# Routing products in groups of eight tokens, all their 0/1 matrices made on VectorE

## The chip, the core and the metric

The kernel runs on one core of one Trainium2 chip. The metric is the device time of one execution in microseconds (us), taken as the median of several runs. Beside it stands one profiled execution, in which the start and the duration of every instruction were recorded; all rows below come from that one.

## The reference

The program computes two transformer blocks on 256 tokens of width 1024. Only the last part of the second block matters here, a mixture of 16384 small experts. For every token and each of 8 heads, two top-16 searches over 128 keys give candidate pairs, the best 16 pairs name experts by a first index `e // 128` and a second index `e % 128`, and a softmax gives each its weight g.

```python
def peer(xn, w_query, sub_keys, expert_u, expert_v):
    ...
        s1, i1 = lax.top_k(s[:, :, 0], PEER_TOPK)
        s2, i2 = lax.top_k(s[:, :, 1], PEER_TOPK)
        ...
        sc, ci = lax.top_k(cand, PEER_TOPK)
        e = (jnp.take_along_axis(i1, ci // PEER_TOPK, axis=-1) * N_KEYS
             + jnp.take_along_axis(i2, ci % PEER_TOPK, axis=-1))
        g = jax.nn.softmax(sc, axis=-1)
        u = expert_u[e]
        act = jax.nn.gelu(jnp.einsum('td,thkd->thk', xb, u).astype(jnp.float32))
        return jnp.einsum('thk,thkd->td', (g * act).astype(xb.dtype), expert_v[e])
```

## The kernel before

The kernel gathers no experts. It computes `gelu(x . u)` for all 16384 experts and all 256 tokens, multiplies by a weight that is zero for experts not chosen, and multiplies the result with all rows of `expert_v`. An f32 product is made of three TensorE passes over numbers split in two parts, a rounded part (`hh`, `wh`) and its remainder (`hl`, `wl`); that is `mm3`.

The work around the change, in order of time:

- **The expert_u units.** `expert_u` comes in 64 units of 256 experts, `u_unit(u)`. A unit has two halves; each half needs one raw 128x1024 tile from a DMA on SyncE's queue, a rounded copy `wh` by ScalarE (line 124) and a remainder `wl` by VectorE (line 130). Then TensorE runs 24 matmuls of 256 columns for each half into the PSUM tile `mid`, 48 a unit. `raw`, `wh` and `wl` have four buffers each, `mid` has two. After a unit, `u_done` applies gelu on ScalarE (line 1010) and stores to `acts0` (units 0 to 31) or `acts1` (units 32 to 63).
- **Routing.** During units 0 to 31 VectorE also ranks the keys. `select_(tb)` ends, for each 128 tokens, with the first index `f1` and the second index `f2` of each chosen expert (lines 938 to 941) and the weight `gw`; TensorE transposes the three (line 945), and ScalarE stores them as `key1`, `key2` and `gwt`, one column a token. `gwt` holds the weight as a sum of three bf16 parts.
- **The table.** `weighted()` is a generator that runs inside units 32 to 63: after every 12 matmuls the unit yields, and each time `next(table)` goes one step on, with one step more after every 12. For a token it makes two bf16 matrices over its 128 chosen pairs: `m2`, 1 where the second index equals the column, and `m1`, the weight where the first index equals the column (`eq`, the 0/1 matrix of line 1071, times `gwt`, line 1073). Three bf16 matmuls of 128 columns (one for each part of the weight), the products, give the token's 128x128 table of weights in a PSUM bank `acc` of four tokens. Of four bank-sized PSUM buffers `acc` in rotation each is emptied by VectorE, which multiplies it into `acts0` (line 1055) and into the units of `acts1` that are done (line 1058), and by ScalarE, which copies it to the units that are still to come (line 1060). Those are multiplied when the unit is done (lines 1012 and 1013).
- **Sizes before.** `eq` and `m1` are made for four tokens an operation. `m2` is made for one token an operation, for three tokens in four by GpSimd (line 1080, the compare in f32) and for the fourth by VectorE (line 1078). A step of the table issues the products of two tokens.
- **The expert_v units.** `v_units` multiplies the 64 units of `acts` with `expert_v`, into the four `acc` buffers.

TensorE's order is the order of the code: `in_line` chains all matmuls. On the other engines a scheduler sets the order from the program's dependences. `m1` and `m2` of a token are made ahead: 12 tokens of `m1` and 8 tokens of `m2` fit in their buffers.

Of the kernel before, what the change touches and what calls it, by code (L numbers as in the profile page):

```python
# [9 lines left out]
F32 = mybir.dt.float32  # L10
F32R = mybir.dt.float32r
BF16 = mybir.dt.bfloat16
I32 = mybir.dt.int32
U32 = mybir.dt.uint32
AF = mybir.ActivationFunctionType
OP = mybir.AluOpType
# [4 lines left out]
P = 128  # L21
S = 256
# [9 lines left out]
HALF = 32  # L32
WBUFS = 4
RBUFS = 4
GAP = 120

SCRATCH = 8192


C_CAUS = 0  # L40
# [39 lines left out]
def block_kernel(ctx: ExitStack, tc: tile.TileContext, a, out, dbg=None):  # L80
    nc = tc.nc
    vec, act, pe, pool = nc.vector, nc.scalar, nc.tensor, nc.gpsimd
# [60 lines left out]
    def matmul(p, x, y, start, stop):  # L143
        in_line(pe.matmul(p, x, y, start=start, stop=stop))  # L144
# [40 lines left out]
    def acc(shape):  # L185
        return ps.tile(shape, F32, name="acc", bufs=4)
# [4 lines left out]
    def tps(shape):  # L191
        return ps.tile(shape, F32, name="tps", bufs=2)
# [330 lines left out]
    i50, i128 = tok[:, :NCAND], tok[:, NCAND:]  # L523
# [18 lines left out]
    for bits in (8, 9, 9, 24):  # L542
        e = 2.0 ** (np.floor(np.log2(abs(rest))) - bits + 1)
        c = float(np.float32(np.round(rest / e) * e))
# [241 lines left out]
    for g0 in (0, 4):  # L786
        p = acc([P, 4, TB, 64])
        for gi in range(4):
            g = g0 + gi
# [3 lines left out]
    p = tps([P, TB, 2])  # L793
# [56 lines left out]
    ranked, done, keys = {}, set(), []  # L850
# [41 lines left out]
    def select_(tb):  # L892

        hv, hi = best[tb]
        hf = pq.tile([P, 8, 2, 16], F32, name="hf")
        turn_of(vec.tensor_scalar(hf[:, :, 0, :], hi[:, :, 0, :], 128.0, None, op0=OP.mult))
        vec.tensor_copy(hf[:, :, 1, :], hi[:, :, 1, :])
        cand = pq.tile([P, 8, NCAND], F32, name="cand")
        ecand = pq.tile([P, 8, NCAND], F32, name="ecand")
        for dst, src in ((cand, hv), (ecand, hf)):  # L900
            for o, i0, r, c in STAIR:
                i = vec.tensor_tensor(dst[:, :, o:o + r * c].rearrange("p h (r c) -> p h r c", c=c),
                                      src[:, :, 0, i0:i0 + r].unsqueeze(3).to_broadcast([P, 8, r, c]),
                                      src[:, :, 1, 0:c].unsqueeze(2).to_broadcast([P, 8, r, c]), op=OP.add)
            yield 2.0
        turns[0] = i
        sc = pq.tile([P, 8, 16], F32, name="sc16")
        pos = pq.tile([P, 8, 16], U32, name="pos")
        posf = pq.tile([P, 8, 16], F32, name="posf")
        ef = pq.tile([P, 8, 16], F32, name="ef")  # L910
        gw = pq.tile([P, 8, 16], F32, name="gw")
        gs = pq.tile([P, 8], F32, name="gs")
        for h in range(8):
            i = best16(sc[:, h, :], pos[:, h, :], cand[:, h, :], NCAND, True)
            if h % 2:
                turns[0] = i
                yield 1.8
        vec.tensor_tensor(gw, sc, sc[:, :, 0:1].to_broadcast([P, 8, 16]), op=OP.subtract)
        act.activation(gw, gw, AF.Exp)
        vec.tensor_copy(posf, pos)  # L920
        for h in range(0, 8, 2):
            eq = pq.tile([P, 2, 16, NCAND], F32, name="eq", bufs=1)
            shape = [P, 2, 16, NCAND]
            turn_of(vec.tensor_tensor(eq, i50.unsqueeze(1).unsqueeze(1).to_broadcast(shape),
                                      posf[:, h:h + 2, :].unsqueeze(3).to_broadcast(shape), op=OP.is_equal))
            yield 1.8
            vec.tensor_tensor(eq, eq, ecand[:, h:h + 2, :].unsqueeze(2).to_broadcast(shape), op=OP.mult)
            yield 1.8
            turns[0] = vec.tensor_reduce(ef[:, h:h + 2, :], eq, axis=AX.X, op=OP.add)
            yield 1.8  # L930
        vec.tensor_reduce(gs, gw, axis=AX.X, op=OP.add)
        vec.reciprocal(gs, gs)
        vec.tensor_tensor(gw, gw, gs.unsqueeze(2).to_broadcast([P, 8, 16]), op=OP.mult)
        ei = pq.tile([P, 8, 16], I32, name="ei")
        e1 = pq.tile([P, 8, 16], I32, name="e1")
        f1 = pq.tile([P, 8, 16], F32, name="f1")
        f2 = pq.tile([P, 8, 16], F32, name="f2")
        vec.tensor_copy(ei, ef)
        vec.tensor_scalar(e1, ei, 7, None, op0=OP.logical_shift_right)
        vec.tensor_copy(f1, e1)  # L940
        turns[0] = vec.scalar_tensor_tensor(f2, f1, -128.0, ef, op0=OP.mult, op1=OP.add)
        yield 2.0
        p = tps([P, 4, P])
        for n, src in enumerate((f1, f2, gw)):
            turn(p[:, n, :], src.rearrange("p h k -> p (h k)"))
        t = slice(tb * P, (tb + 1) * P)
        key1, key2, gwt = keys

        def twice(v):
            return v.unsqueeze(2).to_broadcast([P, P, 2])  # L950

        act.activation(key1[:, t, :], twice(p[:, 0, :]), AF.Copy)
        act.activation(key2[:, t], p[:, 1, :], AF.Copy)  # L953

        rest = pq.tile([P, 8, 16], F32, name="f1").rearrange("p h k -> p (h k)")
        act.activation(gwt[:, t, 0, :], twice(p[:, 2, :]), AF.Copy)
        vec.tensor_tensor(rest, p[:, 2, :], gwt[:, t, 0, 0], op=OP.subtract)
        act.activation(gwt[:, t, 1, :], twice(rest), AF.Copy)
        turns[0] = vec.tensor_tensor(rest, rest, gwt[:, t, 1, 0], op=OP.subtract)
        act.activation(gwt[:, t, 2, :], twice(rest), AF.Copy)  # L960
        yield 0.0
# [39 lines left out]
    acts = [pk.tile([P, 2 * HALF, S], F32, name="acts0")]  # L1001
    NU = NCHUNK // 2
    mixed_in = [0]
    gelus = [0]
# [11 lines left out]
    def u_unit(u):  # L1016
# [2 lines left out]

    abs_ = ExitStack()  # L1020
    ab = abs_.enter_context(tc.tile_pool(name="ab", bufs=1, reuse_waits="tile"))
    keys += [ab.tile([P, S, 2], BF16, name="key1"), ab.tile([P, S], F32, name="key2"),
             ab.tile([P, S, 3, 2], BF16, name="gwt")]
    key1, key2, gwt = keys
    i128b = ab.tile([P, P], BF16, name="i128b")
# [10 lines left out]
    acts.append(pk2.tile([P, 2 * HALF, S], F32, name="acts1"))  # L1036

    def weighted():
        ready = []
        banks = {}  # L1040

        def products(t, m1, m2):
            j = t // 4
            if t % 4 == 0:
                banks[j] = acc([P, 4, P])
            p = banks[j]
            for n in range(3):
                matmul(p[:, t % 4, :], m2, m1[:, n, :], n == 0, n == 2)
            if t % 4 < 3:
                return  # L1050
            ts = slice(4 * j, 4 * j + 4)
            k = 2 * (gelus[0] - HALF)
            pv = p.rearrange("p t c -> p c t")
            g = acts[0][:, :, ts]
            vec.tensor_tensor(g, g, pv[:, :P // 2, :], op=OP.mult)
            if k:
                g = acts[1][:, :k, ts]
                vec.tensor_tensor(g, g, pv[:, P // 2:P // 2 + k, :], op=OP.mult)
            if k < P // 2:
                act.activation(acts[1][:, k:, ts], pv[:, P // 2 + k:, :], AF.Copy)  # L1060
            mixed_in[0] = j + 1

        def by_twos(v):
            return v.rearrange("p t (k i) -> p t k i", i=2)

        for t in range(S):
            if t % 4 == 0:
                eq = ab.tile([P, 4, P], BF16, name="eq", bufs=1)
                m1 = ab.tile([P, 4, 3, P], BF16, name="m1", bufs=3)
                ts = slice(t, t + 4)  # L1070
                vec.tensor_tensor(by_twos(eq), by_twos(i128b.unsqueeze(1).to_broadcast([P, 4, P])),
                                  key1[:, ts, :].unsqueeze(2).to_broadcast([P, 4, P // 2, 2]), op=OP.is_equal)
                vec.tensor_tensor(m1.rearrange("p t n (k i) -> p t n k i", i=2),
                                  eq.rearrange("p t (k i) -> p t k i", i=2).unsqueeze(2).to_broadcast([P, 4, 3, P // 2, 2]),
                                  gwt[:, ts, :, :].unsqueeze(3).to_broadcast([P, 4, 3, P // 2, 2]), op=OP.mult)
            m2 = ab.tile([P, P], BF16, name="m2", bufs=8)
            if t % 4 == 3:
                vec.tensor_scalar(m2, i128b, key2[:, t:t + 1], None, op0=OP.is_equal)
            else:
                pool.tensor_scalar(m2, i128, key2[:, t:t + 1], None, op0=OP.is_equal)  # L1080
            ready.append((t, m1[:, t % 4], m2))
            if len(ready) > 4:
                products(*ready.pop(0))
            if t % 2:
                yield
        while ready:
            products(*ready.pop(0))
            if len(ready) % 2 == 0:
                yield

    table = weighted()
    steps = 0
# [10 lines left out]
    pv = late_pools.enter_context(tc.tile_pool(name="pv", bufs=1, reuse_waits="tile"))  # L1103
# [126 lines left out]
```

## Time and profile before

| | |
|---|---|
| runs, us | 1322.88, 1324.47, 1325.99 |
| median, us | 1324.47 |
| profiled execution, us | 1322.9, its span 1321.1 |
| TensorE clock granted, mean | 0.996 |
| busy: TensorE, VectorE, ScalarE, GpSimd | 97%, 71%, 52%, 31% |
| stage with products | 740 to 953 us of the span |

The span is the time from the first to the last instruction of the profiled execution; its own time is 1.8 us longer. A matmul's duration in the trace overlaps with its neighbours', so the pace of TensorE is read from the distance of two starts, not from durations. The same holds, to a lesser degree, for VectorE.

### The profile page before, as it was taken

What the parts mean: (1) busy time and instruction counts of PE and PEld (TensorE: products, weight loads), DVE (VectorE), ACT (ScalarE), POOL (GpSimd) and SP (SyncE); (2) the same over time, 40 slices, a digit from 0 to 9 for tenths busy, and PEclk for the clock granted to TensorE, in tenths of its full rate; (3) what the DMA queues carried; (4) which work ended last, traced back from release to release, by engine and by line L of the source; (5) the groups of instructions that cost most, each with busy time, mean ns of one, the idle gap of its engine ahead of it and who ended that gap; (6) DMA issues with size and microseconds to landing.
All of it is one profiled execution on the core that took longest, in us unless ns stands there. A gap on an engine that the chain in (4) does not pass through costs nothing.

```text
span 1321.1 us, 22724 instructions
## 1 busy us (share of the span) xinstructions
PE 1287.6 (97%) x8580; PEld 1144.6 (87%) x8580; DVE 932.0 (71%) x1924; ACT 682.7 (52%) x1046; POOL 405.4 (31%) x295
## 2 busy tenths in 40 slices
PE   6999999999998999999999999999999999999997
PEld 5788987899976777999999999999988888888885
DVE  6666777333357795799799699999955555555555
ACT  5576647455544655455564444444444444444443
POOL 3321335222244335300010499999700000000001
PEclk9999999999999999999999999999999999999999
DMA  8554565666645325456766544444476666666662
GB/s 287 169 174 129 183 201 168 215 192 191 191 139 188 113 80 178 126 155 181 226 188 197 172 145 146 147 142 149 154 231 195 194 192 193 194 195 195 194 192 81
DMA packets 64191, 230.65 MB, mean 175 GB/s; under 512 B 7280, under 2 KB 7696, under 8 KB 63952
## 3 DMA queue, kind: packets, MB, share of 16 engines
q1 hardware_dynamic: 61632, 221.03, 54.2%
q0 software_dynamic: 1728, 6.07, 1.3%
q10 hardware_dynamic: 720, 2.10, 0.4%
q8 instruction: 67, 1.10, 0.3%
q14 instruction: 44, 0.36, 0.1%
HBM read 227.07 MB, written 2.10 MB: 173 GB/s over the span
## 4 chain that ended last, share of the span: by engine, by line
PE 89%; DVE 5%; issue 3%; ACT 1%; DMA 1%; POOL 1%; SPq 0%; POOLq 0%; ACTq 0%; DVEq 0%
PE acc L144 52%; PE mid L144 35%; PE tps L154 2%; DVE wl L130 1%; DMA x<-in_x_dram 1%; POOL wl L130 1%; PE tps L144 1%; DVE cnat L339 0%; DVE rope_t L337 0%; DVE at_s L366 0%; ACT wh L124 0%; DVE ny L243 0%; DVE hl L183 0%; DVE rope_t L338 0%; DVE at_s L358 0%
## 5 line engine op out<-in xcount | busy, mean ns | idle before, releaser
L124 ACT ACTIVATE wh<-raw 128x1024 fp32r<-128x1024 f32 (+2 forms) x422 | 440.0, 1049 | 363.1 <-PE mid L144 161.8
L130 DVE TENSOR_TENSOR wl<-raw,wh 128x1024 fp32r<-128x1024 f32 (+1 forms) x350 | 443.7, 1269 | 216.4 <-ACT wh L124 214.0
L144 PE MATMUL mid<-hh,wh 128*128 128x256 f32 x1280 | 365.7, 286 | 0.0
L144 PE MATMUL mid<-hh,wl 128*128 128x256 f32 x1280 | 355.7, 278 | 0.0
L144 PE MATMUL mid<-hl,wh 128*128 128x256 f32 x1280 | 354.3, 277 | 0.0
L130 POOL TENSOR_TENSOR wl<-raw,wh 128x1024 fp32r<-128x1024 f32 (+3 forms) x72 | 177.5, 2475 | 323.9 <-ACT wh L124 273.0
L1080 POOL TENSOR_SCALAR m<-tok,key 128x128 bf16<-128x128 f32 x192 | 206.2, 1092 | 201.7 <-ACT key L953 120.4
L144 PEld LDWEIGHTS mid<-hl,wh 128*128 128x128 f32 x1280 | 241.2, 188 | 0.4
L144 PEld LDWEIGHTS mid<-hh,wh 128*128 128x128 f32 x1280 | 240.9, 188 | 0.4
L144 PEld LDWEIGHTS mid<-hh,wl 128*128 128x128 f32 x1280 | 240.4, 188 | 0.2
L144 PE MATMUL acc<-wl,ah 128*128 128x512 f32 x512 | 199.2, 389 | 0.0
L144 PE MATMUL acc<-wh,ah 128*128 128x512 f32 x512 | 199.2, 389 | 0.0
L144 PE MATMUL acc<-wh,al 128*128 128x512 f32 x512 | 199.2, 389 | 0.0
L144 PE MATMUL acc<-wh,hh 128*128 128x512 f32 (+2 forms) x288 | 115.8, 402 | 2.9 <-ACT hh L182 2.6
L144 PEld LDWEIGHTS acc<-wh,ah 128*128 128x128 f32 x512 | 96.1, 188 | 20.0
L144 PE MATMUL acc<-wl,hh 128*128 128x512 f32 (+2 forms) x288 | 112.2, 390 | 1.3 <-DVE wl L130 0.7
L144 PEld LDWEIGHTS acc<-wh,al 128*128 128x128 f32 x512 | 96.1, 188 | 20.0
L144 PEld LDWEIGHTS acc<-wl,ah 128*128 128x128 f32 x512 | 96.1, 188 | 19.8
L144 PE MATMUL acc<-wh,hl 128*128 128x512 f32 (+2 forms) x288 | 112.4, 390 | 0.8 <-DVE hl L183 0.6
L1138 POOL TENSOR_TENSOR hh<-hh,hl 128x512 f32<-128x512 f32 x4 | 5.1, 1284 | 344.9 <-ACT hl L1137 344.9
L182 ACT ACTIVATE ah<-acts 128x512 fp32r<-128x512 f32 x64 | 40.3, 632 | 88.8 <-PE acc L144 88.8
L183 DVE TENSOR_TENSOR al<-acts,ah 128x512 fp32r<-128x512 f32 x64 | 44.3, 693 | 52.0 <-ACT ah L182 52.0
(267 smaller groups left out, 1750.9 us busy)
## 6 DMA issues: line engine op xcount, KB each, us to landing
raw<-in_expert_u_dram SPq DMA_DIRECT2D x128, 512.0 KB, 3.8
raw<-in_expert_v_dram SPq DMA_DIRECT2D x128, 512.0 KB, 4.4
raw<-in_w_down_dram SPq DMA_DIRECT2D x32, 512.0 KB, 4.4
raw<-in_w_up_dram SPq DMA_DIRECT2D x24, 512.0 KB, 4.7
raw<-in_w_in_dram SPq DMA_DIRECT2D x20, 512.0 KB, 4.5
raw<-in_w_gate_dram SPq DMA_DIRECT2D x16, 512.0 KB, 4.6
raw<-in_w_out_dram SPq DMA_DIRECT2D x16, 512.0 KB, 4.4
raw<-in_w_in_n_dram SPq DMA_DIRECT2D x12, 512.0 KB, 4.5
```

The lines of the kernel that those rows point to most:

```text
L124: i = act.activation(h[:, :n], raw[:, :n], AF.Copy)
L130: last_split[0] = eng.tensor_tensor(l[:, :n], raw[:, :n], h[:, :n].bitcast(F32), op=OP.subtract)
L144: in_line(pe.matmul(p, x, y, start=start, stop=stop))
L154: in_line(pe.transpose(out, src, ident))
L182: turned_[0] = act.activation(h, p, AF.Copy)
L183: vec.tensor_tensor(l, p, h.bitcast(F32), op=OP.subtract)
L1080: pool.tensor_scalar(m2, i128, key2[:, t:t + 1], None, op0=OP.is_equal)
L1138: pool.tensor_tensor(y[:, tb, c], y[:, tb, c], gfin[:, c], op=OP.mult)
```

## The change

The table works in groups of eight tokens. VectorE makes the 0/1 matrices of all tokens, `eq` from `key1` and `m2` from `key2`, each in one operation of 8x128 columns for eight tokens, and `m1` in one operation of 8x384 columns; GpSimd has no part in it. `key2` is stored like `key1`, as bf16 with each value twice. A group's three operations stand in three steps of the table, a fourth step is empty, and the next group's first step issues the 24 products of the group before, back to back. `m1` and `m2` have two buffers of eight tokens, `eq` has one. The room for it comes from two sizes: `GAP`, a filler tile, and `SCRATCH`, the scratch space of the transfers that GpSimd issues.

```diff
-GAP = 120
-
-SCRATCH = 8192
+GAP = 8
+
+SCRATCH = 4096
...
-        act.activation(key2[:, t], p[:, 1, :], AF.Copy)
+        act.activation(key2[:, t, :], twice(p[:, 1, :]), AF.Copy)
...
-            for n in range(3):
-                matmul(p[:, t % 4, :], m2, m1[:, n, :], n == 0, n == 2)
-            if t % 4 < 3:
-                return
...
+        def products(t0, m1, m2):
+            for j in range(t0 // 4, (t0 + T) // 4):
+                p = acc([P, 4, P])
+                for t in range(4 * j, 4 * j + 4):
+                    for n in range(3):
+                        matmul(p[:, t % 4, :], m2[:, t - t0, :], m1[:, t - t0, n, :], n == 0, n == 2)
...
-            m2 = ab.tile([P, P], BF16, name="m2", bufs=8)
-            if t % 4 == 3:
-                vec.tensor_scalar(m2, i128b, key2[:, t:t + 1], None, op0=OP.is_equal)
-            else:
-                pool.tensor_scalar(m2, i128, key2[:, t:t + 1], None, op0=OP.is_equal)
-            ready.append((t, m1[:, t % 4], m2))
-            if len(ready) > 4:
-                products(*ready.pop(0))
-            if t % 2:
-                yield
...
+        def equal(dst, key, ts):
+            vec.tensor_tensor(by_twos(dst), by_twos(i128b.unsqueeze(1).to_broadcast([P, T, P])),
+                              key[:, ts, :].unsqueeze(2).to_broadcast([P, T, P // 2, 2]), op=OP.is_equal)
+
+        made = None
+        for t0 in range(0, S, T):
+            ts = slice(t0, t0 + T)
+            if made:
+                products(*made)
+            eq = ab.tile([P, T, P], BF16, name="eq", bufs=1)
+            equal(eq, key1, ts)
+            yield
+            m2 = ab.tile([P, T, P], BF16, name="m2", bufs=2)
+            equal(m2, key2, ts)
+            yield
+            m1 = ab.tile([P, T, 3, P], BF16, name="m1", bufs=2)
+            vec.tensor_tensor(m1.rearrange("p t n (k i) -> p t n k i", i=2),
+                              by_twos(eq).unsqueeze(2).to_broadcast([P, T, 3, P // 2, 2]),
+                              gwt[:, ts, :, :].unsqueeze(3).to_broadcast([P, T, 3, P // 2, 2]), op=OP.mult)
+            made = (t0, m1, m2)
+            yield
+            yield
+        products(*made)
+        yield
```

In the changed kernel the lines after the diff's first part are numbered differently: 1063 is `equal` (`eq` and `m2`), 1078 is `m1`, 1051, 1054 and 1056 are the three that were 1055, 1058 and 1060.

Over the whole program, TensorE's order before has 118 unbroken runs of products, 108 of six and 10 of twelve; afterwards it has 32 runs of 24. All other matmuls stand in the same order. On TensorE, in unit 33, the end of the first run of products before (`acc`, from `m1` and `m2`) and what follows it:

```order
L144 MATMUL acc_8256<-m1_8215,m2_8218 128x128
L144 LDWEIGHTS m2_8220
L144 MATMUL acc_8256<-m1_8215,m2_8220 128x128
L144 LDWEIGHTS m2_8220
L144 MATMUL acc_8256<-m1_8215,m2_8220 128x128
L144 LDWEIGHTS m2_8220
L144 MATMUL acc_8256<-m1_8215,m2_8220 128x128
L144 MATMUL mid_8201<-hh_4200,wh_8197 128x256
```

and, in the first run of the changed kernel, the place where the fourth token ends and the fifth begins:

```order
L144 MATMUL acc_8282<-m1_8242,m2_8228 128x128
L144 LDWEIGHTS m2_8228
L144 MATMUL acc_8282<-m1_8242,m2_8228 128x128
L144 LDWEIGHTS m2_8228
L144 MATMUL acc_8298<-m1_8242,m2_8228 128x128
L144 LDWEIGHTS m2_8228
```

Where the unit's matmuls (`mid`) came back after two tokens, the next bank's products now follow without a break.

On VectorE, in the middle of the stage with products, two rounds of the table before (1055 and 1058 empty a bank, 1078 is the fourth token's `m2`, 1073 is `m1`, 1071 is `eq`, 1013 is a unit's product, 130 is `wl`):

```order
L1055 TENSOR_TENSOR acts_5882<-acts_5882,acc 128x64x4
L1058 TENSOR_TENSOR acts_8188<-acts_8188,acc 128x18x4
L1078 TENSOR_SCALAR m_9444<-i128b,key_5887 128x128
L1073 TENSOR_TENSOR m_9465<-eq,gwt 128x1536
L130 TENSOR_TENSOR wl<-raw,wh 128x1024
L1071 TENSOR_TENSOR eq<-i128b,key_5886 128x512
L1013 TENSOR_TENSOR acts_8188<-mid,acts_8188 128x2x80
L1055 TENSOR_TENSOR acts_5882<-acts_5882,acc 128x64x4
L1058 TENSOR_TENSOR acts_8188<-acts_8188,acc 128x20x4
L1078 TENSOR_SCALAR m_9496<-i128b,key_5887 128x128
L1073 TENSOR_TENSOR m_9520<-eq,gwt 128x1536
L1071 TENSOR_TENSOR eq<-i128b,key_5886 128x512
```

and the same stretch now:

```order
L1051 TENSOR_TENSOR acts_5882<-acts_5882,acc 128x64x4
L1054 TENSOR_TENSOR acts_8188<-acts_8188,acc 128x18x4
L1063 TENSOR_TENSOR m_9296<-i128b,key_5887 128x1024
L1078 TENSOR_TENSOR m_9313<-eq,gwt 128x3072
L130 TENSOR_TENSOR wl<-raw,wh 128x1024
L1063 TENSOR_TENSOR eq<-i128b,key_5886 128x1024
L1013 TENSOR_TENSOR acts_8188<-mid,acts_8188 128x2x80
L1051 TENSOR_TENSOR acts_5882<-acts_5882,acc 128x64x4
L1054 TENSOR_TENSOR acts_8188<-acts_8188,acc 128x20x4
L130 TENSOR_TENSOR wl<-raw,wh 128x1024
L1051 TENSOR_TENSOR acts_5882<-acts_5882,acc 128x64x4
L1054 TENSOR_TENSOR acts_8188<-acts_8188,acc 128x20x4
```

The three table operations of eight tokens stand once for two bank emptyings, the two long ones together between two `wl`.

On VectorE too, but earlier, at the end of routing for the second 128 tokens, before (938 to 941 make the indices that TensorE transposes next):

```order
L929 TENSOR_REDUCE ef_7347<-eq_7909 128x32
L130 TENSOR_TENSOR wl_8063<-raw_8060,wh_8062 128x1024
L938 CAST ei_7978<-ef_7347 128x128
L130 TENSOR_TENSOR wl_8069<-raw_8066,wh_8068 128x1024
L939 TENSOR_SCALAR e1_7979<-ei_7978 128x128
L940 CAST f1_7980<-e1_7979 128x128
L941 SCALAR_TENSOR_TENSOR f2_7981<-f1_7980,ef_7347 128x128
L130 TENSOR_TENSOR wl_8125<-raw_8122,wh_8124 128x1024
L130 TENSOR_TENSOR wl_8131<-raw_8128,wh_8130 128x1024
```

and now:

```order
L929 TENSOR_REDUCE ef_7347<-eq_7909 128x32
L130 TENSOR_TENSOR wl_8069<-raw_8066,wh_8068 128x1024
L938 CAST ei_7978<-ef_7347 128x128
L130 TENSOR_TENSOR wl_8125<-raw_8122,wh_8124 128x1024
L939 TENSOR_SCALAR e1_7979<-ei_7978 128x128
L940 CAST f1_7980<-e1_7979 128x128
L941 SCALAR_TENSOR_TENSOR f2_7981<-f1_7980,ef_7347 128x128
L130 TENSOR_TENSOR wl_8131<-raw_8128,wh_8130 128x1024
```

The split `wl_8125` stood behind 941 and now stands ahead of 939. Between the indices of the first and of the second 128 tokens VectorE has 4 `eq` (four tokens each), 2 `m2` (one token each) and 3 `m1` (four tokens each) before, and 3 `eq`, 2 `m2` and 2 `m1`, all of eight tokens, now.

## Rows read from the trace of the kernel before

**Rows 1.** The page, part 1: busy us, share of the span, instructions.

```profile
PE 1287.6 (97%) x8580; PEld 1144.6 (87%) x8580; DVE 932.0 (71%) x1924; ACT 682.7 (52%) x1046; POOL 405.4 (31%) x295
```

**Rows 2.** Window with products: length, busy PE, PEld, DVE, ACT, POOL, clock, DMA, GB/s.

```profile
740.00:953.00 213.00, 213.00 (x2176) 208.79 (x2175) 202.50 (x396) 94.48 (x178) 200.93 (x186) 1.00 0.49 147
```

**Rows 3.** Waits between 740 and 953 us: total, times, longest.

```profile
ACT wh L124 <- PE mid L144: 73.8, 47, 2.4
ACT acts L1060 <- DVE acts L1058: 40.4, 28, 2.1
DVE acts L1055 <- PE acc L144: 7.7, 19, 1.3
```

**Rows 4.** Timeline of PE: start, duration; unit matmuls without and with products.

```profile
722.41 0.28 PE L144 MATMUL mid<-hh,wh 128*128 128x256 f32 x1
...
723.77 0.28 PE L144 MATMUL mid<-hh,wh 128*128 128x256 f32 x1
...
756.08 0.28 PE L144 MATMUL mid<-hh,wl 128*128 128x256 f32 x1
756.20 0.84 PE L144 MATMUL acc<-m,m 128*128 128x128 bf16 x12
756.85 0.36 PE L144 MATMUL mid<-hh,wh 128*128 128x256 f32 x1
...
758.20 0.28 PE L144 MATMUL mid<-hh,wl 128*128 128x256 f32 x1
...
758.64 0.36 PE L144 MATMUL mid<-hh,wh 128*128 128x256 f32 x1
...
801.88 0.51 PE L144 MATMUL acc<-m,m 128*128 128x128 bf16 x6
...
810.82 0.51 PE L144 MATMUL acc<-m,m 128*128 128x128 bf16 x6
```

**Rows 5.** Timeline of DVE in the middle of the stage: start, duration.

```profile
801.67 1.22 DVE L130 TENSOR_TENSOR wl<-raw,wh 128x1024 fp32r<-128x1024 f32 x1
802.81 0.23 DVE L1058 TENSOR_TENSOR acts<-acts,acc 128x72 f32<-128x72 f32 x1
...
803.15 0.42 DVE L1071 TENSOR_TENSOR eq<-i128b,key 128x512 bf16<-128x512 bf16 x1
803.49 0.42 DVE L1055 TENSOR_TENSOR acts<-acts,acc 128x256 f32<-128x256 f32 x1
...
803.96 0.25 DVE L1078 TENSOR_SCALAR m<-i128b,key 128x128 bf16<-128x128 bf16 x1
804.12 0.95 DVE L1073 TENSOR_TENSOR m<-eq,gwt 128x1536 bf16<-128x1536 bf16 x1
804.99 1.32 DVE L130 TENSOR_TENSOR wl<-raw,wh 128x1024 fp32r<-128x1024 f32 x1
```

**Rows 6.** Groups of the whole span, by shape: busy us, mean ns.

```profile
L1080 POOL TENSOR_SCALAR m<-tok,key 128x128 bf16<-128x128 f32 x192 | 206.2, 1092 | 201.7 <-ACT key L953 120.4 <-PE acc L144 81.3
...
L924 DVE TENSOR_TENSOR eq<-tok,posf 128x1600 f32<-128x1600 f32 x8 | 14.5, 1819 | 0.0
```

**Rows 7.** Timelines of DVE, ACT and PE where routing ends: start, duration, idle before.

```profile
720.53 1.22 DVE L130 TENSOR_TENSOR wl<-raw,wh 128x1024 fp32r<-128x1024 f32 x1
721.67 0.22 DVE L939 TENSOR_SCALAR e<-ei 128x128 int32<-128x128 int32 x1
722.19 0.29 DVE L941 SCALAR_TENSOR_TENSOR f<-f,ef 128x128 f32<-128x128 f32 x1
723.25 1.23 DVE L130 TENSOR_TENSOR wl<-raw,wh 128x1024 fp32r<-128x1024 f32 x1 [0.77 <-ACT wh L124]
...
722.16 1.06 ACT L124 ACTIVATE wh<-raw 128x1024 fp32r<-128x1024 f32 x1 [1.18 <-PE mid L144]
...
724.80 0.38 PE L154 MATMUL tps<-ident,f 128*128 128x128 f32 x2
```

**Rows 8.** Timeline of POOL behind its first eight transfers: start, duration, idle before.

```profile
11.52 1.85 POOL L130 TENSOR_TENSOR wl<-raw,wh 128x768 fp32r<-128x768 f32 x1 [5.83 <-ACT wh L124]
```

More of the change, by code (lines that the diff above doesn't have):

```diff
@@ L1021, in block_kernel @@
     ab = abs_.enter_context(tc.tile_pool(name="ab", bufs=1, reuse_waits="tile"))
-    keys += [ab.tile([P, S, 2], BF16, name="key1"), ab.tile([P, S], F32, name="key2"),
+    keys += [ab.tile([P, S, 2], BF16, name="key1"), ab.tile([P, S, 2], BF16, name="key2"),
              ab.tile([P, S, 3, 2], BF16, name="gwt")]
@@ L1038, in weighted @@
     def weighted():
[L1039 to L1046, printed above, removed]
-            for n in range(3):
-                matmul(p[:, t % 4, :], m2, m1[:, n, :], n == 0, n == 2)
-            if t % 4 < 3:
-                return
[L1051 to L1061, printed above, removed]
+        T = 8
@@ new lines, in products @@
+        def products(t0, m1, m2):
[4 more added lines that the diff above has]
+                        matmul(p[:, t % 4, :], m2[:, t - t0, :], m1[:, t - t0, n, :], n == 0, n == 2)
+                ts = slice(4 * j, 4 * j + 4)
+                k = 2 * (gelus[0] - HALF)
+                pv = p.rearrange("p t c -> p c t")
+                g = acts[0][:, :, ts]
+                vec.tensor_tensor(g, g, pv[:, :P // 2, :], op=OP.mult)
+                if k:
+                    g = acts[1][:, :k, ts]
+                    vec.tensor_tensor(g, g, pv[:, P // 2:P // 2 + k, :], op=OP.mult)
+                if k < P // 2:
+                    act.activation(acts[1][:, k:, ts], pv[:, P // 2 + k:, :], AF.Copy)
+                mixed_in[0] = j + 1
@@ L1063, in by_twos @@
         def by_twos(v):
             return v.rearrange("p t (k i) -> p t k i", i=2)
[L1066 to L1075, printed above, removed]
-            m2 = ab.tile([P, P], BF16, name="m2", bufs=8)
-            if t % 4 == 3:
-                vec.tensor_scalar(m2, i128b, key2[:, t:t + 1], None, op0=OP.is_equal)
-            else:
-                pool.tensor_scalar(m2, i128, key2[:, t:t + 1], None, op0=OP.is_equal)
-            ready.append((t, m1[:, t % 4], m2))
-            if len(ready) > 4:
-                products(*ready.pop(0))
-            if t % 2:
-                yield
@@ L1086, in weighted @@
[L1086 to L1089, printed above, removed]
+        def equal(dst, key, ts):
[19 more added lines that the diff above has]
+            yield
```

## The prediction

> **What bounds the kernel now.** I read the busy times first: TensorE is busy 97% of the span and no other engine over 71% [rows 1], so a change pays only where it shortens TensorE's own work or a wait of it. Then the window of the stage with products, 740 to 953 us: TensorE 213.0 of 213.0 us at the full clock (2.4 GHz), VectorE 202.5, GpSimd 200.9 [rows 2]. Three engines are nearly full, so it must be asked which one sets the pace. The waits tell: in this stage TensorE is never the one that waits. ScalarE waits 47 times for TensorE to give a weight buffer back, and VectorE 7.7 us for products to empty [rows 3]. The busy matmul rows alone would not prove it, since their durations overlap, but the starts do: five runs of six products with 12 unit matmuls each begin between 801.88 and 810.82, so a period takes 8.94 / 5 = 1.788 us [rows 4]. TensorE sets the pace, with VectorE 10.5 us of 213 behind it.
>
> **The gain: fewer returns from bf16 to f32.** Without products 12 unit matmuls take 723.77 - 722.41 = 1.36 us [rows 4]. From the last unit matmul ahead of a run to the first behind it there are 0.77 us with twelve products (756.08 to 756.85) and 0.44 us with six (758.20 to 758.64), so six more products cost 0.33 us, 0.055 us each [rows 4]. A period of six products is then 1.36 + 0.33 = 1.69 us, and the trace has 1.788: each run costs 0.095 us beyond its matmuls (0.085 to 0.105 with the rounding of the rows). The stage's length agrees: between its first and its last product the order has 117 x 12 unit matmuls and 768 products, 117 x 1.36 + 768 x 0.055 + 118 x 0.095 = 212.6 us, and the stage has 213 [rows 2]. A run of twelve pays it once, not twice, so it belongs to the run, not to the product; nothing in the trace has a run of 24. The order has 118 runs before and 32 after, with the same 768 products: 86 x 0.095 = 8.2 us less, 7.3 to 9.0. All of it lies on the path that sets the end, since TensorE runs without a gap from here to the end.
>
> **VectorE.** Its work must stay under TensorE's new pace. Read from start to start, `eq` of 512 elements takes 803.49 - 803.15 = 0.34 us, `m1` of 1536 takes 0.87, one `m2` 0.16, `wl` 1.14 [rows 5]. Two sizes of the same kind give 0.52 ns an element and 0.07 us fixed; so 1024 elements are 0.60 us and 3072 are 1.67. Eight tokens cost 2 x (0.34 + 0.87 + 0.16) = 2.74 us before and 0.60 + 0.60 + 1.67 = 2.87 after: 0.13 more, for 32 groups 4.2 us. All evictions and splits stay. That VectorE takes over GpSimd's 192 matrices (206 us there [rows 6]) for 4 us is the point of the large operations: eight tokens share one fixed cost. The bounds: the line could hold exactly (4.2 us), or the larger operation could lose the rate of two elements a cycle and run like the f32 compare over 1600 elements, 1.82 us or 1.14 ns an element [rows 6]; then a group takes 5120 x 1.14 ns = 5.8 us, 2.97 more than 2.87, 95 us in all. I take the line: the operands have the same type and the same innermost pairs as line 1071, which is on it. Below it lies at most what GpSimd's company costs VectorE now: `wl` takes 1.22 us at 801.67 and 1.32 at 804.99 [rows 5], 0.1 us for some of the 59 splits. TensorE's stage becomes 213 - 8.2 = 204.8 us and VectorE's need 202.5 + 4.2 = 206.7 by its busy time. That reads like a tie, but busy time counts the last 0.08 us of an operation in which the next one already runs or could (0.42 us lasting, 0.34 to the next start [rows 5]); from starts alone the need is near 195 us. So I cost the move to VectorE at nothing, covered by TensorE; with that cover gone it is 2 us.
>
> On this the Trainium skill has a rule that speaks against the change: in "VectorE: DVE Perf Modes", section "The perf-mode tier table", a bf16 `tensor_scalar` may run four elements a cycle and `tensor_tensor` only two, so the 1024 elements of `m2` would cost about 0.27 us more (an estimate from that page) in the form chosen here. By that sentence alone VectorE would lose 32 x 0.27 = 8.5 us against a `tensor_scalar` that could serve eight tokens, but there the key is one column for each token. The rows have one token at 0.16 us, eight 1.3 us, so here the fixed cost decides and the rule does not.
>
> **What queues behind the longer operations.** VectorE now stands in the order two bank evictions, `m2` and `m1` (2.27 us together), and then a split. A `wl` can come some 4 us late. TensorE needs it only later: buffers come round after four halves of a unit, a half takes about 3.6 us (two 12-matmul steps of 1.79), so a freed buffer is needed again three halves later, 10.7 us, of which ScalarE takes 1.06 and VectorE 1.23 [rows 7]: 8.4 us are left. ScalarE's copies wait for VectorE's evictions, up to 2.1 us before [rows 3], and `wh` is queued behind them; the same 8.4 us cover it, as they cover both delays together (4 + 3). `m1` is made a whole group ahead of its use, about 6.4 us; only for the last three groups does the order put it into the period just before, about 5 us of VectorE work (two evictions of two operations, a split, `m2`, a unit's product, `m1`; an estimate from [rows 5]) ahead of 48 unit matmuls of 4 x 1.36 = 5.4 us. Tight, but covered. Price of these: nothing.
>
> **One place where TensorE will wait.** At the end of routing VectorE has more to do in front of line 941. One part is table work since the first 128 tokens, 6.3 us against 4.3 by the prices above. The other is the split that now stands ahead of line 939: before, it started at 723.25, held by its `wh` that ScalarE made from 722.16 to 723.22, behind TensorE [rows 7]. It cannot start earlier, so 939 starts at 723.25 + 1.14 = 724.39 in place of 721.67, and 941 (0.52 behind it, 0.29 long) ends at 725.2. TensorE transposes the indices at 724.80, the second index about 0.1 later [rows 7]: it waits about 0.35 us. If all 2.0 us of additional table work come on top, the split starts at 720.53 + 2.0 + 1.14 = 723.67 and the wait is 0.8; if ScalarE's copy comes earlier than before, there is none. I take 0.4.
>
> **What costs nothing.** GpSimd's 192 operations end; nobody but the products waited for them. The wider copy of `key2` is 0.1 us twice on a ScalarE that idles. The smaller scratch could hold GpSimd's transfers back; behind the first eight of them GpSimd idles 5.83 us for ScalarE [rows 8], which hides as much.
>
> **The sum.** -8.2 + 0.4 = -7.8 us. The profiled execution took 1322.9 us, span 1321.1 and 1.8 around it; that gives 1315.1. It lies 1.6 below the median of 1324.47, so against the median I expect 1316.7.
>
> **The rivals.**
> - VectorE becomes the pace. For it: 206.7 against 204.8 by busy time. Against it: starts. It costs 1.9 us: 1318.6. Still faster.
> - VectorE's idle stays (the slower end). Its order is fixed; the 7.7 us in which it waits for products and the other 2.8 may recur, since two evictions now come at once and then nothing for 5 us. The stage would need 202.5 + 4.2 + 10.5 = 217.2 us, 4.2 over the 213 of before: 1324.5 + 4.2 + 0.4 = 1329.1. It decides from the point where `m1` lags by more than the 6.4 us it is ahead. Against it: a late VectorE does not wait for products, they are there.
> - The return costs more after a long run, or the saving is a cost of products after all (the change does not do what it says): 1324.5 + 0.4 = 1324.9, no change. Against it: the run of twelve.
> - The large operations lose their rate: 202.5 + 4.2 + 95 = 302 us of VectorE, 97 over TensorE's: 1414.
> - The Trainium skill, "SBUF — State Buffer", section "Terms", says that VectorE and GpSimd lock each other out of a shared port pair. The rows show the mechanism faintly on VectorE (0.1 us on a split); with GpSimd silent VectorE gains some of the 4.2 us back. That makes the first two rivals less likely and changes no sum.
>
> **How the numbers follow.** The forecast (1315 to 1318.5) has 0.70, VectorE as the pace 0.11, no change 0.09, VectorE's idle 0.07, the lost rate 0.03. A measurement tells about 0.2%, 2.6 us, from no change, so faster means under 1321.8. Faster is 0.70 + 0.11, less 0.01 for a median at the edge: 0.80; same 0.11; slower 0.09. The range goes from the largest saving, 9.0 without a wait (1315.5), less 1.6 for the spread between runs, 1314, up to 1322, which leaves out most of the last three cases (0.19).
>
> **What would show it.** In the profile after: runs of 24 products of about 1.33 us; 12 unit matmuls between them at 1.36; no TensorE wait in the stage but one near 725 us of some 0.4; the stage 8 us shorter; line 1063 near 0.68 us long and line 1078 near 1.75; VectorE busy some 200 of 205 us. A TensorE wait for `m1` in each group would show VectorE as the pace; a longer first unit matmul behind the run of 24 would show the return dearer than I take it.

## The result, and the profile after

The changed kernel took 1333.5 us, the median of five runs (1333.02 to 1333.92), against 1324.47 for the kernel before (five runs, 1322.88 to 1326.75): a ratio of 1.0061, 95% interval 1.0049 to 1.0073. It is slower by 9 us where 8 us of gain were forecast, and it lies outside the range.

The profile of the changed kernel, part 1 of its page, in the form of [rows 1]:

```profile
PE 1301.2 (98%) x8580; PEld 1159.1 (87%) x8580; DVE 927.8 (70%) x1828; ACT 683.8 (51%) x1046; POOL 199.4 (15%) x103
```

VectorE and GpSimd have less to do, as the change says. TensorE has the same 8580 matmuls and is busy 13.6 us longer. So the loss is not a new wait of TensorE: its own matmuls take longer. Where, the starts on its timeline tell. The table below follows the same matmuls through both kernels; each number is the distance of two starts of matmuls.

| stretch of TensorE's order | before, us | after, us | difference |
|---|---|---|---|
| TensorE's first matmul to the first of `expert_u` | 549.26 | 552.40 | +3.1 |
| to the index transposes of the second 128 tokens | 165.33 | 172.20 | +6.9 |
| these transposes and the next unit matmul | 0.45 | 0.72 | +0.3 |
| to the first matmul of `expert_v` (all products lie here) | 238.64 | 239.28 | +0.6 |
| to the last matmul | 347.95 | 347.98 | 0.0 |

The second line holds no product and, on TensorE, nothing that the change touches, yet it costs 6.9 us. The window from 650 to 700 us, in which TensorE does nothing but unit matmuls, shows why. The rows count the instructions on `mid` alone, so the 0.00 of VectorE does not mean that it idles. First the kernel before (length, busy PE with its count, PEld, DVE, ACT, clock, DMA, GB/s):

```profile
650.00:700.00 50.00, 49.92 (x441) 49.74 (x440) 0.00 (x0) 5.64 (x10) 1.00 0.63 193
```

and the changed kernel:

```profile
650.00:700.00 50.00, 49.92 (x421) 49.73 (x420) 0.00 (x0) 5.24 (x9) 1.00 0.59 180
```

At the same granted clock and without a gap, 421 unit matmuls fit where 441 did: 50 / 421 = 0.1188 us each in place of 50 / 441 = 0.1134. The timeline of the changed kernel shows it directly (start, duration; twelve matmuls lie between the first and the second row, then come the last unit matmul ahead of a run of products, the run, and the first one behind it):

```profile
731.77 0.28 PE L144 MATMUL mid<-hl,wh 128*128 128x256 f32 x1
...
733.20 0.28 PE L144 MATMUL mid<-hl,wh 128*128 128x256 f32 x1
...
753.86 0.28 PE L144 MATMUL mid<-hh,wl 128*128 128x256 f32 x1
753.98 1.51 PE L144 MATMUL acc<-m,m 128*128 128x128 bf16 x24
755.30 0.36 PE L144 MATMUL mid<-hh,wh 128*128 128x256 f32 x1
```

Twelve take 1.43 us where they took 1.36 [rows 4]; the durations are still 0.28, so only the starts give it away. The run of 24 products, 1.32 us, is what was forecast.

VectorE's table operations came out as forecast too (groups between 754 and 963 us; busy us, mean ns):

```profile
L1078 DVE TENSOR_TENSOR m<-eq,gwt 128x3072 bf16<-128x3072 bf16 x30 | 52.5, 1749 | 0.0
L1063 DVE TENSOR_TENSOR m<-i128b,key 128x1024 bf16<-128x1024 bf16 x30 | 20.5, 682 | 0.0
L1063 DVE TENSOR_TENSOR eq<-i128b,key 128x1024 bf16<-128x1024 bf16 x29 | 19.8, 682 | 0.0
```

And the stage with products, from the transposes to `expert_v`, as a window of the kernel before (length, busy PE, PEld, DVE, ACT, POOL, clock, DMA, GB/s):

```profile
725.25:963.89 238.64, 238.64 (x2401) 234.43 (x2400) 217.28 (x413) 109.36 (x202) 200.93 (x186) 1.00 0.50 152
```

The same stretch of the changed kernel:

```profile
735.59:974.87 239.28, 239.28 (x2402) 237.84 (x2400) 212.38 (x319) 109.33 (x202) 0.00 (x0) 1.00 0.50 150
```

TensorE fills both without a wait. In `expert_v`, where TensorE holds `ah` and `al` and the weights are the moving operand of 512 columns, nothing changed: 884 matmuls in 200 us in both kernels. The window (length, busy PE, clock, DMA, GB/s) of the changed kernel:

```profile
1050.00:1250.00 200.00, 200.00 (x884) 1.00 0.65 194
```

and of the kernel before:

```profile
1050.00:1250.00 200.00, 200.00 (x884) 1.00 0.64 194
```

But `ah` and `al` are allocated from the same end as the weights, so that in this stage the change moves both operands together.

The first stretch of the table, +3.1 us, has 256-column matmuls of the same kind in the two blocks; part of what they lose is given back at a wait, `tps` for `cnat` (TensorE's waits between 300 and 560 us: total, times, longest), before

```profile
PE tps L154 <- DVE cnat L339: 3.2, 1, 3.2
```

and after

```profile
PE tps L154 <- DVE cnat L339: 1.1, 2, 0.9
```

More follows the wait of 3.2 us in the kernel before: the granted clock falls to 0.50, the 1.2 GHz level, for 3.4 us (columns as in [rows 2]):

```profile
420.50:423.90 3.40, 3.40 (x11) 2.73 (x9) 3.40 (x8) 0.60 (x1) 0.00 (x0) 0.50 0.86 258
```

Eight matmuls of 512 columns take 3.49 us there (starts from 420.49 to 423.98), the next eight 1.84 (to 425.82). The changed kernel waits 0.9 us at most at this place, and its clock stays at 1.00 from 300 to 560 us. So the 3.1 us are what is left of a larger loss: 3.1 + 2.1 + 1.65, some 6.9 us (an estimate from these rows).

### The profile page after: what moved, and what is told of

Read it like the earlier page. It is cut to its first block, busy times and chain, and to the rows that moved or that the text cites. A ratio compares the mean times of both kernels' runs of the same rounds, so it can differ in the third digit from the quotient of the medians.

```text
span 1331.8 us, 22204 instructions
## 1 busy us (share of the span) xinstructions
PE 1301.2 (98%) x8580; PEld 1159.1 (87%) x8580; DVE 927.8 (70%) x1828; ACT 683.8 (51%) x1046; POOL 199.4 (15%) x103
## 4 chain that ended last, share of the span: by engine, by line
PE 90%; DVE 5%; issue 3%; ACT 1%; DMA 1%; POOL 1%; SPq 0%; POOLq 0%; ACTq 0%; DVEq 0%
PE acc L144 52%; PE mid L144 36%; PE tps L154 2%; DVE wl L130 1%; DMA x<-in_x_dram 1%; POOL wl L130 1%; PE tps L144 1%; DVE rope_t L337 0%; DVE at_s L366 0%; DVE cnat L339 0%; ACT wh L124 0%; DVE ny L243 0%; DVE hl L183 0%; DVE rope_t L338 0%; DVE at_s L358 0%
## 5 line engine op out<-in xcount | busy, mean ns | idle before, releaser
L144 PE MATMUL mid<-hh,wl 128*128 128x256 f32 x1280 | 361.0, 282 | 0.0
L144 PE MATMUL mid<-hl,wh 128*128 128x256 f32 x1280 | 360.8, 282 | 0.0
L144 PEld LDWEIGHTS acc<-wh,hh 128*128 128x128 f32 x288 | 54.7, 190 | 18.6 <-ACT hh L182 5.1
L144 PEld LDWEIGHTS acc<-wh,hl 128*128 128x128 f32 x288 | 54.7, 190 | 15.0 <-DVE hl L183 4.0
```

## The experiments

The order of the matmuls outside the stage with products is the same in both kernels, and so is the work. What the change moves for all of them is where the tiles lie. `SCRATCH` and `GAP` stand ahead of the buffers `raw`, `wh` and `wl`, which begin at byte SCRATCH + 4640 + 4 x GAP of each partition, as the built program places them: 13312 before, 8768 after. `hh` and `hl` are allocated from the other end, behind a filler `gapr`, and did not move (212928 and 221120). The `wh` and `wl` of the units lie multiples of 1024 behind that beginning.

**Layout or table?** Four kernels; the edits:

```diff
@@ e1, against the kernel before @@
-GAP = 120
+GAP = 8
@@ e2, against the changed kernel @@
-GAP = 8
+GAP = 120
-SCRATCH = 4096
+SCRATCH = 3072
@@ e3, against the kernel before @@
-SCRATCH = 8192
+SCRATCH = 4096
@@ e4, against the changed kernel @@
-GAP = 8
+GAP = 24
```

> The kernel before with GAP = 8 alone: every tile of the left side moves down by 448 bytes, so the weight buffers start at 12864 (576 over a multiple of 1024) in place of 13312 (a multiple of 1024), as in the changed kernel, whose ring starts at 8768, also 576 over. The order on all engines stays the same. Theory, layout: the unit matmuls slow from 0.1133 to about 0.119 us, as in the changed kernel; 64 units x 0.26 us = 16.5 us and up to 3 us in earlier stages: 1341 to 1344 us. Rival, table (the groups of eight slow TensorE): unit matmuls stay at 0.1133, 1324.5 us.

> The changed kernel with SCRATCH = 3072 and GAP = 120: the ring starts at 8192, a multiple of 1024, and the order on all engines is that of the changed kernel. Theory, layout: unit matmuls return to 0.1133 us, 1333.5 - 16.5 = 1317 us or 1 to 2 less, and the table keeps its saving of about 8 us. Rival, table: 1333.5 us, unit matmuls at 0.119.

> The kernel before with SCRATCH = 4096 alone: the ring starts at 9216, still a multiple of 1024, and GpSimd's transfers have half the scratch. Theory, layout by the remainder: no change, 1324.5 us, unit matmuls 0.1133. Rival, the smaller scratch itself (or the absolute address) costs: up to 1333 to 1341 us.

> The changed kernel with GAP = 24: the ring starts at 8832, a multiple of 128 but 640 over one of 1024. If a multiple of 128 is enough: unit matmuls at 0.1133, 1317 us. If it takes 512 or 1024: 0.119, 1333.5 us. Anything between says that several distances matter. The rival, table, gives 1333.5 in every case.

Measured beside 1323.81 for the kernel before: e1 1339.62 (ratio 1.0113, 1.0088 to 1.0138), e2 1315.36 (0.9931, 0.9907 to 0.9955), e3 1323.32 (0.9991, 0.9976 to 1.0007), e4 1328.3 (1.0034, 1.0023 to 1.0046). The window from 650 to 700 us in e1:

```profile
650.00:700.00 50.00, 49.92 (x421) 49.73 (x420) 0.00 (x0) 5.24 (x9) 1.00 0.61 185
```

and in e2:

```profile
650.00:700.00 50.00, 49.92 (x440) 49.74 (x440) 0.00 (x0) 5.22 (x9) 1.00 0.64 199
```

The kernel before, with nothing but a smaller filler, gets the 421 of the changed kernel and becomes the slowest of these; the changed kernel, with its buffers moved back to a multiple of 1024, gets 440 and is faster than both. So the layout makes the loss, not the table, and of the two sizes it is `GAP`: alone it costs the kernel before 15.8 us, and the smaller scratch space alone costs nothing (e3). e4 is in between, which the next runs had to explain.

**Which tile, and address or distance?** At first I took the address of `wh` and `wl` themselves for the cause. The edits (`padw` is a filler between `raw` and `wh`):

```diff
@@ e5, against the kernel before @@
-GAP = 120
+GAP = 8
-    gapr.tile([P, 8], F32, name="gapr")
+    gapr.tile([P, 120], F32, name="gapr")
@@ e6, against the kernel before @@
-    gapr.tile([P, 8], F32, name="gapr")
+    gapr.tile([P, 248], F32, name="gapr")
@@ e7, against the changed kernel @@
-SCRATCH = 4096
+SCRATCH = 3072
+    ring.tile([P, 112], F32, name="padw"); ...
@@ e8, against e2 @@
+    ring.tile([P, 144], F32, name="padw"); ...
```

> The kernel before with the filler GAP at 8 and, on the other side of the memory, a second filler (gapr) of 120 columns in place of 8: both the weight tiles (raw, wh, wl) and the moving tiles (hh, hl) lie 448 bytes lower, so their distance from each other is that of the kernel before, and the weight tiles lie at 576 beyond a multiple of 1024 as in the slow run of the kernel before with GAP = 8. If the weight tiles' own address decides: unit matmuls of 256 columns at 0.119 us from start to start, about 1339 us. If the distance between weights and moving operand decides: 0.1133 us, about 1324 us.

> The kernel before with only the filler on the moving tiles' side widened from 8 to 248 columns: hh and hl start at a multiple of 1024 bytes in place of 960 beyond one; the weight tiles stay at their multiple of 1024. If only the weight tiles' address matters: 0.1133 us a unit matmul and 1324 us. If the moving operand's address matters as the weights' does: under 0.1133, down to some 0.108, which would be 1309 us or less over the 3072 matmuls of the units.

> The changed kernel with SCRATCH at 3072 (GAP 8 as it is) and 448 bytes of filler behind the raw buffers: raw lies at 576 beyond a multiple of 1024 as in the changed kernel, wh and wl and all that follows at a multiple of 1024. If TensorE's reading of wh and wl is what the address slows: 0.1133 us a unit matmul and 1315 us. If the raw buffers' address (transfers writing, ScalarE and VectorE reading) is what matters: 0.119 us and 1333 us.

> The opposite of the run before: SCRATCH at 3072, GAP at 120, raw at a multiple of 1024 and 576 bytes of filler behind it, so that wh and wl and all that follows lie at 576 beyond one. If the address of wh and wl decides: 0.119 us a unit matmul and about 1332 us. If that of raw does: 0.1133 us and 1315 us.

Measured beside 1323.65: e5 1325.21 (1.0014, 1.0002 to 1.0026), e6 1340.42 (1.0127, 1.011 to 1.0144), e7 1316.54 (0.9946, 0.9929 to 0.9963), e8 1333.94 (1.0074, 1.0057 to 1.0091). e7 and e8 settle the tile: with only `raw` at the bad place nothing is lost, with `wh` and `wl` there and `raw` at the good one all of it is. e5 refutes my first theory: the weights lie at the bad address, but `hh` and `hl` were moved along, and all but 1.6 us of the loss is gone (in its profile TensorE waits 1.2 us for GpSimd's matrices, which it does not in the kernel before). e6 missed both of its expectations: with `hh` and `hl` moved to a round address and the weights where they always were, the window holds

```profile
650.00:700.00 50.00, 49.92 (x416) 49.73 (x416) 0.00 (x0) 5.23 (x9) 1.00 0.61 181
```

416, the fewest so far. What counts is the distance between the stationary tiles (`wh`, `wl`) and the moving ones (`hh`, `hl`). That a matmul and the next load of weights are under way together stands on the timelines of the changed kernel (start, duration). A matmul on PE:

```profile
699.73 0.28 PE L144 MATMUL mid<-hl,wh 128*128 128x256 f32 x1
```

and the next load of weights, on PEld:

```profile
699.74 0.19 PEld L144 LDWEIGHTS mid<-hh,wl 128*128 128x128 f32 x1
```

The load starts 0.01 us after the start of the matmul before it, and both last longer than the 0.12 us from start to start.

**Which distances?** Four more, all in the layout of e2 with only `gapr` changed, so that the weights stay and `hh` and `hl` move (with all other tiles of that end, none of which TensorE reads in the units):

```diff
-    gapr.tile([P, 8], F32, name="gapr")
@@ e9 @@
+    gapr.tile([P, 16], F32, name="gapr")
@@ e10 @@
@@ e11 @@
+    gapr.tile([P, 56], F32, name="gapr")
@@ e12 @@
+    gapr.tile([P, 72], F32, name="gapr")
```

> The changed kernel in the layout that gave 1315 us (SCRATCH 3072, GAP 120), with the filler gapr at 16 columns in place of 8, so that only hh and hl move: the weight tiles lie 96 bytes beyond the moving tiles, counted modulo 512, in place of 64. Measured so far by that distance: 0 gives 0.1195 us a unit matmul, 64 gives 0.1133, 128 gives 0.119, 192 gives 0.118. If the distance decides with a slope: about 0.116 and 1324 us. If it goes by steps of 64 bytes: 0.1133 and 1315 us.

> As the run before, with gapr left out: distance 32 bytes modulo 512, between 0 (0.1195 us) and 64 (0.1133 us). With a slope: about 0.116 and 1324 us. By steps of 64 bytes: 0.1195 as at 0 and 1335 us.

> gapr at 56 columns: distance 256 bytes modulo 512. If the pattern repeats every 256 bytes it is that of distance 0: 0.1195 us and 1335 us. If it repeats only after 512 bytes, the value is not known beforehand; at 0.110 or less the kernel would come near 1305 us.

> gapr at 72 columns: distance 320 bytes modulo 512. If the pattern repeats every 256 bytes it is that of distance 64: 0.1133 us and 1315 us. If it repeats only after 512 bytes, the value is not known beforehand, between 0.107 and 0.120.

Measured beside 1323.53: e9 1329.28 (1.0043, 1.0027 to 1.0059), e10 1332.06 (1.0059, 1.0043 to 1.0075), e11 1336.08 (1.0088, 1.0058 to 1.0118), e12 1314.94 (0.9943, 0.992 to 0.9965). e11 and e12 fall as a pattern that repeats every 256 bytes wants it. e9 and e10 miss both of their figures: 32 bytes to either side of 64 are neither half way nor free, most of the loss is there at once. All layouts by distance modulo 256 bytes (address of `wh` less address of `hh`), with the count of unit matmuls between 650 and 700 us:

| distance | kernels | matmuls in 50 us | us each |
|---|---|---|---|
| 0 | e6, e11 | 416 | 0.120 |
| 32 | e10 | 423 | 0.118 |
| 64 | before, e2, e3, e5, e7, e12 | 437 to 441 | 0.113 to 0.114 |
| 96 | e9 | 424 | 0.118 |
| 128 | after, e1, e8 | 421 | 0.119 |
| 192 | e4 | 424 | 0.118 |

Of the distances tried, 64 is the only good one. The kernel before stood there; the changed kernel stands at 128.

**Is that all, and whose is the gain?** e13 is the changed kernel with its `SCRATCH` of 4096 and only the two fillers taken out, which gives the distance 64 with the buffers beginning at 8736, no round address. e14 and e15 take the layout of e2 and give the runs of products back, at the same operations on VectorE: two runs of twelve a group (four tokens in its first and its third step), or four of six (two tokens in each step, the edit shown).

```diff
@@ e13, against the changed kernel @@
-GAP = 8
...
-    gap = ctx.enter_context(tc.tile_pool(name="gap", bufs=1))
-    gap.tile([P, GAP], F32, name="gap")
...
-    gapr = ctx.enter_context(tc.tile_pool(name="gapr", bufs=1, side="right"))
-    gapr.tile([P, 8], F32, name="gapr")
@@ e15, against e2 @@
-        def products(t0, m1, m2):
-            for j in range(t0 // 4, (t0 + T) // 4):
-                p = acc([P, 4, P])
-                for t in range(4 * j, 4 * j + 4):
...
+        def products(t0, m1, m2, i):
+            N = 2
+            for t in range(t0 + N * i, t0 + N * i + N):
+                if t % 4 == 0:
+                    bank[0] = acc([P, 4, P])
...
-                products(*made)
+                products(*made, 0)
...
+                products(*made, 1)
...
+                products(*made, 2)
...
+                products(*last, 3)
```

> The changed kernel with SCRATCH left at 4096 and both filler tiles left out: raw, wh and wl move down by 32 bytes and hh and hl up by 32, which makes the distance 64 bytes modulo 256 again; all addresses are multiples of 32 only. If the distance modulo 256 is all that slowed the changed kernel: 0.1133 us a unit matmul and 1315 us. If the weight tiles must also begin at a round address, or the smaller scratch holds something back: over 1320 us.

> The changed kernel in the layout that gave 1315 us (SCRATCH 3072, GAP 120), the same 0/1 matrices in the same operations of eight tokens, but the products of a group issued as two runs of twelve in its first and its third step: 63 runs in place of 32. If each run costs 0.095 us beyond its matmuls: 31 x 0.095 = 2.9 us more, 1318.3. If the gain was VectorE's or GpSimd's and not the runs': 1315.4, no change.

> The same with two tokens in each of the four steps: 118 runs, 108 of six and 10 of twelve as in the kernel before, while VectorE still makes all matrices in operations of eight tokens and GpSimd makes none. If each run costs 0.095 us: 86 x 0.095 = 8.2 us more than with 32 runs, 1323.5. If the gain was not the runs': 1315.4.

Measured beside 1324.71: e13 1315.79 (0.9945, 0.9926 to 0.9965), e14 1318.79 (0.9963, 0.9949 to 0.9977), e15 1324.04 (0.9999, 0.9985 to 1.0012). e13 gets the full gain, so neither the smaller scratch nor a round address of the weights has a part in it. The stage with products between the same two matmuls, as a window (columns as above), in e2 with 32 runs:

```profile
727.44:958.07 230.63, 230.43 (x2401) 229.15 (x2400) 211.66 (x319) 109.19 (x202) 0.00 (x0) 1.00 0.53 156
```

in e14 with 63:

```profile
725.95:959.75 233.80, 233.80 (x2401) 231.56 (x2400) 211.34 (x319) 107.23 (x202) 0.00 (x0) 1.00 0.52 154
```

and in e15 with 118:

```profile
728.01:966.61 238.60, 238.60 (x2402) 234.40 (x2400) 211.73 (x319) 107.23 (x202) 0.00 (x0) 1.00 0.50 151
```

The 31 additional runs of e14 add 3.17 us, 0.102 each, the 86 of e15 7.97 us, 0.093 each. With 118 runs and all matrices on VectorE the stage is as long as that of the kernel before, 238.64: the move from GpSimd to VectorE is worth nothing that these runs show (e15's ratio, 0.9985 to 1.0012), and the gain is the runs'.

## Why the prediction was wrong, point by point

**The step that failed** is "What costs nothing". "The smaller scratch could hold GpSimd's transfers back" weighs one of the two sizes, and only for what it holds; the other, `GAP`, was put at nothing without a word, and I never asked what lies behind them. Both move every `wh` and `wl`, which TensorE reads in all 3072 unit matmuls and in others before: `SCRATCH` by 4096 bytes, a multiple of 256, which cost nothing (e3), and `GAP` by 448, which cost 15.8 us (e1). Beside it, "12 unit matmuls between them at 1.36" took the pace of TensorE for a property of the matmul; it is one of the layout. Against e13, the same kernel with the fillers out, the price is 1333.5 - 1315.79 = 17.7 us: 172.20 - 165.43 = 6.8 us in the units ahead of the transposes, 239.28 - 230.66 = 8.6 in the stage with products, and the rest, some 2.3, before the units, where the first stretch takes 552.40 against 550.06. (e13 has the wait of 3.2 us and the low clock of the kernel before there, so the matmuls themselves lose more than 2.3.) The mechanism is not among the rivals either, so slower had a chance of 0.09.

**The gain** was right for the distance 64, which the prediction took for granted. Forecast were 8.2 us (7.3 to 9.0) for 86 runs at 0.095; its own terms, 1.788 - 1.69, give 0.098 and 8.4 us. The stage went from 238.64 to 230.63 in e2, 8.0 us, and e14 and e15 find 0.102 and 0.093 us a run. At the distance 128 the same 86 runs are worth less. With the old routing table at this distance, in e1, the stage is (columns as in [rows 2])

```profile
736.38:981.75 245.37, 245.37 (x2401) 239.92 (x2400) 217.71 (x413) 109.76 (x202) 193.70 (x186) 1.00 0.50 147
```

and in the changed kernel 239.28, 6.1 us or 0.07 a run; the medians, 1339.62 and 1333.5, say the same. So the +0.6 that the stage lost is 6.7 us for the layout less 6.1 for the runs. At the distance 0 the old and the new routing table, e6 and e11, are 1340.42 - 1336.08 = 4.3 us apart. Why the runs cost less there, no run shows.

**VectorE** was right in its prices, 0.68 and 1.75 us, and in that TensorE stays the pace. In e2's stage TensorE waits for it once (total, times, longest), at 938.93, for the `m1` of one of the last groups, which "Tight, but covered" priced at nothing:

```profile
PE acc L144 <- DVE m L1078: 0.2, 1, 0.2
```

My need of 206.7 us by busy time was too high: the stage has 211.66 us of VectorE in e2 against 217.28 before over the same stretch, less and not 4.2 more. That long operations count the overlap with the next one less often would fit, and so would the splits, a little shorter, and the 2.0 us of table work that now stand ahead of the stage; no run tells them apart. The prices and the single wait refute the rivals of VectorE as the pace and of the lost rate. The rival that its idle stays is refuted as well: in the changed kernel VectorE does wait (waits between 740 and 964 us),

```profile
DVE wl L130 <- ACT wh L124: 13.9, 12, 1.6
DVE acts L1051 <- PE acc L144: 7.7, 15, 0.8
```

21.6 us in two lines, and TensorE never waits for it; in e2 the same two lines come to 18.1 us. The Trainium skill's rule that VectorE and GpSimd lock each other out of a shared port pair ("SBUF — State Buffer", section "Terms") has little to show here: a split lasts 1240 ns on average between 740 and 953 us before, beside GpSimd, and 1219 in the changed kernel with GpSimd silent, 21 ns less, against 1092 for one of GpSimd's operations [rows 6]. That the 21 ns are the lock no run shows. The Trainium skill's rule on four elements a cycle for `tensor_scalar` ("VectorE: DVE Perf Modes", section "The perf-mode tier table") no run here tests; with 19 us of VectorE to spare in e2's stage it could not have moved the time.

**The wait at the transposes** was right: forecast 0.4. From the last unit matmul ahead of them to the first behind, e2 takes 727.23 - 726.46 = 0.77 us (the timeline of PE),

```profile
726.46 0.28 PE L144 MATMUL mid<-hh,wl 128*128 128x256 f32 x1
726.71 0.66 PE L154 MATMUL tps<-ident,f 128*128 128x128 f32 x2
727.20 0.27 PE L154 MATMUL tps<-ident,gw 128*128 128x128 f32 x1
727.23 0.37 PE L144 MATMUL mid<-hh,wh 128*128 128x256 f32 x1
```

against 725.04 - 724.68 = 0.36 before, 0.41 more. The cause is the forecast one: the split ahead of line 939 starts at 725.03, held 0.68 us by its `wh`, and line 941 ends at 726.98, behind the start of the transposes. In the changed kernel, where TensorE comes later, it is 735.39 - 734.74 = 0.65, 0.29 more.

**The sum** of 1316.7 us thus fits the kernel that the text describes, 1315.4 in e2, 1316.5 in e7 and 1315.8 in e13, and not the one that the diff makes. The rival that the return is dearer after a long run, or that the saving belongs to the products, is refuted by e14 and e15: the same products in more runs bring the time back run by run.

What stays open is why 64 bytes are good: no run separates `wh` from `wl`, `hh` from `hl`, or these two from the other tiles that move with them, and the distances 160 and 224 were not tried.

## What to carry to other kernels

A size that makes room is an edit of its own: before it is priced at nothing, list which tiles it moves and which of them an engine reads at the same time. TensorE's pace is to be read from the starts in a stretch that the change does not touch, in the kernel before and after; where it differs there, look at the layout and not at the change. And where TensorE sets the pace, each run of bf16 products between f32 matmuls costs time beyond its matmuls, here 0.09 to 0.10 us at the distance 64 and 0.07 at 128, so longer runs pay.

## What the runs showed of the hardware

- The pace of f32 matmuls of 256 columns, each with its own weight load, went with the distance between stationary and moving tile modulo 256 bytes: 0.113 to 0.114 us at 64, 0.118 at 32, 96 and 192, 0.119 at 128, 0.120 at 0, at a granted clock of 1.00 from 650 to 700 us in every run. Over this kernel that is up to 21 us (1314.94 in e12, 1336.08 in e11).
- The matmuls of 512 columns in `expert_v` kept their pace, 884 or 885 in 200 us in every kernel, but there no run changed the distance. Where 512 columns of `wh` and `wl` meet `hh` and `hl`, in the first stretch, it counts too, and otherwise: 95 of them in a row took 22.17 us before (starts from 179.72 to 201.89), 22.16 in the changed kernel (182.53 to 204.69) and 21.56 in e11 (182.02 to 203.58) and in e6, the shortest at the distance that is worst for 256 columns.
- The absolute address had no effect that a run shows: buffers beginning at 8736 (e13), 12864 (e5) and 13312 (before) gave the good pace alike, 440 or 441 unit matmuls in 50 us, as long as the distance was 64.
- A run of bf16 products between f32 matmuls cost the same beyond its matmuls with 6, 12 and 24 products, 0.09 to 0.10 us at the distance 64; at 128 it was 0.07.
- Behind a wait of 3.2 us TensorE's granted clock was 0.50 (1.2 GHz) for 3.4 us in the kernel before, and eight matmuls of 512 columns took 3.49 us in place of 1.84.
